# A hybrid encoder block on one core: the begin rewritten (V's products split by kind and interleaved, first weights in three loads, high parts of rows on GpSimd)

## The chip, the cores and the metric

The kernel runs on one core of one Trainium2 chip. The metric is the device time of one execution in microseconds; the median of three runs of the kernel before is 1219.09 us (1218.88 to 1220.08).

## The reference

One encoder layer on 1024 tokens of width 1024, all in float32. In outline:

```
u = rms_norm(x, norm1_g)
proj = u @ w_in                 # q, k, v (512 each), cb, cc, ch (512 each), ga, gb (1024 each)
q, k = per-head rms_norm of q, k (8 heads x 64)
y_a = neighbourhood_attention(q, k, v, rpb) @ w_attn_branch   # 8 x 16 window on a 16 x 64 grid
y_b = (cb * conv3(cc * ch)) @ w_conv_branch
x = x + (sigmoid(ga) * y_a + sigmoid(gb) * y_b) @ w_o
x = x + relu(rms_norm(x, norm2_g) @ w_mlp_in)^2 @ w_mlp_out
```

## The kernel before, in words

Float32 products are made of float16 ones. Every operand is written as a high part (rounded to float16, scaled by a power of two) and a low part (what is left), and a product is three TensorE passes: high by high, high by low, low by high (`PASSES`, L464). The high part is one instruction (`ACTIVATE` on ACT, or `TENSOR_SCALAR` on GpSimd), the low part one `SCALAR_TENSOR_TENSOR` on DVE that reads the high part.

**Rows.** The tokens are eight blocks of 128, called rows here and numbered from 0. `norm` (L435) makes a row's `u`: sum of squares on ACT (L438), a short chain of DVE instructions with one root on ACT (`rstd`, L411 to L420), the high part (L442 on GpSimd for rows 1 to 3, L444 on ACT for the others), the low part on DVE (L446). It is a generator, and `ln_step(b, n)` issues the next n pieces of row b. Rows 0 to 2 are transposed by TensorE with copies out of PSUM (`ln_trans`, L448: high part copied by ACT, L456, low by DVE, L458); rows 3 to 7 by a DMA from SP's queue (`ln_turn`, L461). `u16` has four slots, row b uses slot b mod 4.

**Weights.** A `Chunk` (L242) is a slice of the weights: V has two chunks of 256 columns, Q and K one of 512, each in pieces of 512 KB that SP loads into five `raw` buffers (L232; the next load is issued once a piece's low parts are on DVE). `prep` (L252) finds a scale (by largest value or by sum of squares, L263 on ACT), sums it over the partitions with a product by ones (L201) that DVE reads (L204), turns it into a power of two, scales the rows' gains (L279), and then makes the high parts (L310, ACT) and low parts (L301, DVE) piece by piece.

**Order.** The order on each engine is that in which this Python program issues. Two lists of generators are stepped along with TensorE's work: `fg` (`step`, finishing work of rows and units, the s splits) and `bg` (`tick`, the weights' `prep`). `units` counts finished groups of 24 products; several generators wait in this count (`apart`). A unit's results are read out of PSUM when the next unit has been issued (`settle`); for V this is L534 (ACT) and L535 (DVE).

**The begin, L540 to L596.** V's chunk 0 is prepared, then each of rows 0 to 2 gets a group of 24 products with 256 columns (128x256), then the same rows with chunk 1, then rows 3 to 7 one group each with both chunks (128x512). Q's chunk is prepared meanwhile and Q's groups follow directly (L654). Also in this stretch `sforms` (L491) makes, for later use, sums and differences of x's halves: for a pair of rows n and n + 4 ACT scales both (L499), GpSimd does four `TENSOR_TENSOR` (L503), and later ACT and DVE split the result (`s`, L508 and L510). `SFORM` (L489) gives the count of units from which each may be issued.

TensorE's banks are `d` (3), `s` (3) and `o` (2).

Of the kernel before, what the change touches and what calls it, by code (L numbers as in the profile page):

```python
# [52 lines left out]
def encoder_block(ctx: ExitStack, tc: tile.TileContext, x, weights, cols, gqk, rel, masks, out):  # L53
# [128 lines left out]
    def apart(mark, n=3, of=units):  # L182
        while of[0] < mark + n and not forced[0]:
            yield WAIT
# [57 lines left out]
    class Chunk:  # L242


        def __init__(self, kind, widths, tag, rows, half, more):
            self.kind, self.bank = kind, {"V": "o", "Q": "o", "K": "s", "C": "d"}.get(kind)
            self.tag, self.rows, self.widths, self.more = tag, rows, widths, more
            self.offs = []
            self.raw, self.ready, self.half = [], more > 0, half
            self.split = False  # L250

        def prep(self):  # L252
# [5 lines left out]
            if self.kind in "QKCG" or self.half:  # L258
                self.parts = vhome[0][:, 1] if self.half else wsp.tile([128, 2, tot], F16, name="w16_ws", tag="ws")
# [10 lines left out]
                if self.half:  # L270
                    yield
                else:
                    yield from apart(units[0], 2 if self.kind == "Q" else 3)
                yield from all_sum(c, b, bank(self.bank) if self.bank else anybank(), 1e-36, not self.half)
# [8 lines left out]
            if self.half is not None:  # L283
                if not self.half:
                    vhome.append(wsp.tile([128, 2, 2, tot], F16, name="w16_v", tag="ws"))
                self.parts = vhome[0][:, self.half]
            elif self.kind not in "QKCG":
                self.parts = wpool[self.tag].tile([128, 2, tot], F16, name="w16_" + self.tag, tag=self.tag)
# [27 lines left out]
        def largest(self, rm, a, b):  # L316
            o = 0
# [15 lines left out]
            if self.kind != "V":  # L333
                yield from apart(units[0], 3 if self.kind != "O" else 1 + (self is cO[1]))
            yield from all_sum(c, b, bank(self.bank) if self.bank else anybank(), 1e-30, self.kind != "V")
# [112 lines left out]
    def ln_trans(u16, b, dst):  # L448
        for s in range(2):
            pt = bank16("o")  # L450
            for k in range(8):
                T.transpose(pt[:, k * 128:(k + 1) * 128], u16[:, s, k * 128:(k + 1) * 128], ident)
            o = dst[:, s, :, b * 128:(b + 1) * 128]
            i = pt.rearrange("p (k t) -> p k t", k=8)
            if s == 0:
                A.activation(o, i, AF.Copy)  # L456
            else:
                V.tensor_copy(o, i)  # L458

# [25 lines left out]
    ln = [norm(xt[:, b], sq, u16[:, b % 4], at(ys, b), 0 < b < 4) for b in range(8)]  # L485
# [42 lines left out]
    def v_unit(b, j, steps, ticks):  # L528
        ps = bank("ds"[b % 2])
        n, c = (512, 0) if j is None else (256, 256 * j)  # L530

        def post():
            hi, lo = (VT[:, b, s, c:c + n] for s in range(2))
            A.activation(hi, ps[:, :n], AF.Copy, scale=2.0 ** -20)  # L534
            V.scalar_tensor_tensor(lo, ps[:, :n], 2.0 ** -20, hi, op0=OP.mult, op1=OP.subtract)  # L535
        w = vhome[0] if j is None else vhome[0][:, j]
        unit(group(ps[:, :n], [(UT[:, sa, k, b * 128:(b + 1) * 128], w[..., sw, k * 256:(k + 1) * 256])
                               for k in range(8) for sa, sw in PASSES]), post, steps, ticks)
# [1275 lines left out]
```

## Time and profile before

| | |
|---|---|
| median of three runs | 1219.09 us |
| the profiled execution | 1219.86 us, of which its span is 1218.0 us |
| granted TensorE clock | 1.0 throughout |
| PE busy over the span | 98% |
| DVE, ACT, POOL busy over the span | 76%, 63%, 35% |
| chain that ended last, by engine | PE 74%, DVE 15%, ACT 5%, DMA 3%, issue 2% |

PE is TensorE's products, PEld its weight loads, POOL is GpSimd, SP issues DMAs. A row of the timeline gives start, duration, engine, line, operation, output and inputs, shapes, how many such instructions are merged in the row, and in brackets how long the engine was idle before it and what ended this. Where several are merged the duration is that of all. A row of the table by stage gives the stretch, its length, the busy time of PE, PEld, DVE, ACT and POOL, each with its number of instructions, then clock, DMA share and GB/s. A row of the chain that ended last gives start, duration and what was worked on.

### The profile page before, as it was taken

What the parts mean: (1) busy time and instruction counts of PE and PEld (TensorE: products, weight loads), DVE (VectorE), ACT (ScalarE), POOL (GpSimd) and SP (SyncE); (2) the same over time, 40 slices, a digit from 0 to 9 for tenths busy, and PEclk for the clock granted to TensorE, in tenths of its full rate; (3) what the DMA queues carried; (4) which work ended last, traced back from release to release, by engine and by line L of the source; (5) the groups of instructions that cost most, each with busy time, mean ns of one, the idle gap of its engine ahead of it and who ended that gap; (6) DMA issues with size and microseconds to landing.
All of it is one profiled execution on the core that took longest, in us unless ns stands there. A gap on an engine that the chain in (4) does not pass through costs nothing.

```text
span 1218.0 us, 17069 instructions
## 1 busy us (share of the span) xinstructions
PE 1194.1 (98%) x6294; PEld 572.9 (47%) x6294; DVE 931.3 (76%) x1758; ACT 764.4 (63%) x1186; POOL 423.2 (35%) x276
## 2 busy tenths in 40 slices
PE   5999999999999999999999999999999999999998
PEld 4544444454444444444458444444444444444444
DVE  6667878898468686887877665456448989998997
ACT  6786677777545455436668787687776754646440
POOL 1430003231411111101003465655657472553562
PEclk9999999999999999999999999999999999999999
DMA  7558555756651121226095654355375835335302
GB/s 279 106 186 182 113 124 114 154 111 118 133 143 54 51 69 35 70 62 246 19 184 131 208 190 160 129 187 166 129 284 199 314 127 203 143 134 195 104 35 104
DMA packets 170867, 173.35 MB, mean 142 GB/s; under 512 B 131488, under 2 KB 132000, under 8 KB 166688
## 3 DMA queue, kind: packets, MB, share of 16 engines
q1 hardware_dynamic: 170208, 168.07, 47.6%
q10 hardware_dynamic: 576, 4.19, 0.9%
q8 instruction: 49, 0.80, 0.3%
q14 instruction: 34, 0.28, 0.1%
HBM read 102.51 MB, written 37.75 MB: 115 GB/s over the span
## 4 chain that ended last, share of the span: by engine, by line
PE 74%; DVE 15%; ACT 5%; DMA 3%; issue 2%; SPq 0%; POOL 0%; ACTq 0%; DVEq 0%
PE ps_d L210 26%; PE ps_s L210 23%; PE ps_o L210 16%; PE ps_d L911 7%; DVE w_s L1033 2%; PE ps_s L831 1%; PE ps_o L888 1%; DVE w_ws L301 1%; DMA qD<-q 1%; DVE s L510 1%; DVE u L446 1%; DVE sg L1149 1%; DMA u2T<-v 1%; ACT w_ws L263 1%; DVE w_v L301 1%
## 5 line engine op out<-in xcount | busy, mean ns | idle before, releaser
L210 PEld LDWEIGHTS <-ops 128*128 128x128 f16 x1356 | 132.4, 98 | 157.3
L210 PEld LDWEIGHTS <-w 128*128 128x128 f16 x1368 | 132.8, 98 | 140.5 <-DMA u2T<-v 1.0
L911 PE MATMUL ps_d<-uT,w_ws 128*128 128x512 f16 x528 | 125.0, 379 | 0.0
L210 PE MATMUL ps_d<-ops 128*128 128x512 f16 (+1 forms) x528 | 118.3, 374 | 0.0
L1635 ACT ACTIVATE ops<-hf,sc 128x2048 f16<-128x2048 f32 x26 | 52.0, 2002 | 98.5 <-PE ps_o L210 35.9
L210 PE MATMUL ps_s<-ops 128*128 128x512 f16 x492 | 112.9, 379 | 0.0
L1022 POOL TENSOR_TENSOR tsum<-raw 128x512 f32<-128x512 f32 x28 | 45.8, 1648 | 148.9 <-ACT raw L1008 148.9
L210 PEld LDWEIGHTS <-uT 128*128 128x128 f16 x648 | 63.4, 99 | 68.2 <-issue 5.4
L1215 POOL TENSOR_TENSOR as<-as 128x512 f32<-128x512 f32 x56 | 77.5, 1385 | 40.8 <-ACT as L1495 37.5
L210 PEld LDWEIGHTS <-w_s 128*128 128x128 f16 x588 | 56.8, 98 | 69.5 <-DVE w_s L1033 2.0
L210 PE MATMUL ps_d<-u2x,w 128*128 128x512 f16 (+1 forms) x360 | 80.0, 372 | 0.0
L210 PE MATMUL ps_o<-ops 128*128 128x512 f16 x336 | 77.1, 379 | 0.0
L911 PEld LDWEIGHTS <-w_ws 128*128 128x128 f16 x528 | 51.0, 98 | 52.8
L1637 DVE SCALAR_TENSOR_TENSOR ops<-hf,sc,ops 128x2048 f16<-128x2048 f32 x26 | 72.6, 2791 | 3.5 <-ACT ops L1635 3.5
L1008 ACT ACTIVATE raw<-raw,sc 128x256 f32<-128x256 f32 x172 | 71.1, 496 | 1.9 <-DMA raw<-in_weights 1.9
L210 PE MATMUL ps_o<-u2T,w 128*128 128x512 f16 (+1 forms) x324 | 71.7, 371 | 0.0
L1022 POOL TENSOR_TENSOR gsum<-raw 128x512 f32<-128x512 f32 x14 | 19.0, 1377 | 133.8 <-issue 73.7
L1037 ACT ACTIVATE w<-raw,sc 128x512 f16<-128x512 f32 (+1 forms) x28 | 24.7, 929 | 52.3 <-DVE sc L431 52.3
L210 PE MATMUL ps_s<-u2T,w 128*128 128x512 f16 (+1 forms) x252 | 52.7, 359 | 0.0
L854 ACT ACTIVATE sz<-sz,sc 128x384 f32<-128x384 f32 (+1 forms) x64 | 37.4, 584 | 24.3 <-DVE sc L845 12.5
L1528 DVE TENSOR_TENSOR as<-ps_d,as 128x512 f32<-128x512 f32 (+1 forms) x14 | 9.4, 672 | 55.6 <-ACT as L1547 53.5
L310 ACT ACTIVATE w_ws<-raw,sc 128x512 f16<-128x512 f32 (+2 forms) x72 | 41.0, 638 | 15.6 <-DVE sc L279 15.6
(340 smaller groups left out, 2616.8 us busy)
## 6 DMA issues: line engine op xcount, KB each, us to landing
raw<-in_weights SPq DMA_DIRECT2D x89, 512.0 KB, 5.8
hs<-as SPq DMA_DIRECT2D x16, 1792.0 KB, 8.8
hf<-hs SPq DMA_DIRECT2D x26, 1024.0 KB, 6.7
w2x<-in_weights SPq DMA_DIRECT2D x16, 512.0 KB, 8.3
raw<-in_weights SPq DMA_DIRECT2D x16, 384.0 KB, 3.7
xt<-in_x SPq DMA_DIRECT2D x8, 512.0 KB, 10.1
gs<-s ACTq DMA_DIRECT2D x4, 1024.0 KB, 4.6
x<-in_x SPq DMA_DIRECT2D x8, 512.0 KB, 9.7
```

The costliest lines, as they stand in the source:

```text
L210: T.matmul(ps, l, r, start=a, stop=b)
L301: V.scalar_tensor_tensor(lo, self.raw[p][:, o:o + m], sc[:, c:c + 1], hi, op0=OP.mult, op1=OP.subtract)
L310: A.activation(self.parts[:, 0, f + o:f + o + m], self.raw[p][:, o:o + m], AF.Copy, scale=sc[:, c:c + 1])
L854: A.activation(z, z, AF.Exp, scale=-1.0, bias=sc[:, d["mx"]], accum_out=sc[:, d["sm"]])
L911: T.matmul(ps, l, r, start=a, stop=b)
L1008: A.activation(v, v, AF.Copy, scale=sc[:, at(g, 4 * i + k)])
L1022: G.tensor_tensor(t[:, o], a, b, op=OP.add)
L1033: V.scalar_tensor_tensor(o(1), w, sc[:, s], o(0), op0=OP.mult, op1=OP.subtract)
L1037: A.activation(o(0), w, AF.Copy, scale=sc[:, s])
L1215: sub.tensor_tensor(z[o], z[a], z[b], op=op)
L1635: A.activation(P[:, 1, 0], hf, AF.Copy, scale=sc[:, Rs])
L1637: V.scalar_tensor_tensor(P[:, 1, 1], hf, sc[:, Rs], P[:, 1, 0], op0=OP.mult, op1=OP.subtract)
```

## The change

Only the begin is rewritten, with the helpers that it calls.

- The second piece of V's chunk 0 is loaded in two halves (so the first weights come in three loads), and the search for the largest value follows the loads (4 + 2 + 2 slices).
- The begin's order is written out by hand: `turn_row` (half of the former `ln_trans`), `v_part` (high or low parts of some slices), `v_mms` (products of some slices and passes), `v_post`. V's products go by kinds: high by high, low by high and high by low of rows 0, 1, 2 are apart and interleaved with transposes, and three groups (one for each of rows 0, 1, 2) are open in three banks at a time.
- Rows 1 to 7 make their high part on GpSimd (before: rows 1 to 3).
- The norms of rows 4 to 7 are issued ahead of the products of row 3; before, they were issued one by one between the products.
- Q's chunk is pushed once, before the last passes of V's chunk 1, with two ticks ahead of row 3's product; before, it got two ticks at each of three groups.

The core of the diff (left out: the branches of `prep` and `largest` for V that are no longer used, `ln_trans`, and `v_unit`'s half form; `HH`, `HL`, `LH` are the three passes):

```
     def load_into(t, ch, p):
         m = ch.widths[p][0] * ch.widths[p][1]
-        SP.dma_start(t, bass.AP(tensor=weights.tensor, offset=weights.offset + ch.offs[p], ap=[[m, 128], [1, m]]))
+        n = m // (1 + (ch.half == 0 and p == 1))
+        for o in range(0, m, n):
+            SP.dma_start(t[:, o:o + n], bass.AP(tensor=weights.tensor, offset=weights.offset + ch.offs[p] + o,
+                                                ap=[[m, 128], [1, n]]))
...
-    ln = [norm(xt[:, b], sq, u16[:, b % 4], at(ys, b), 0 < b < 4) for b in range(8)]
+    ln = [norm(xt[:, b], sq, u16[:, b % 4], at(ys, b), b > 0) for b in range(8)]
...
+    def turn_row(b, s):
+
+        pt = bank16("o")
+        for k in range(8):
+            T.transpose(pt[:, k * 128:(k + 1) * 128], u16[:, b, s, k * 128:(k + 1) * 128], ident)
+
+        def copy():
+            o, i = UT[:, s, :, b * 128:(b + 1) * 128], pt.rearrange("p (k t) -> p k t", k=8)
+            if s == 0:
+                A.activation(o, i, AF.Copy)
+            else:
+                V.tensor_copy(o, i)
+        return copy
+
+    def v_begin(ch):
+        ch.rm, ch.a, ch.b, ch.s = (cols_of("prep", i) for i in (8, 1, 1, 1))
+        ch.inv = keep()
+
+    def v_sum(ch, c):
+        ch.sum = bank("o")
+        T.matmul(ch.sum[:, 0:1], ones[:, 0:128], c, start=True, stop=True)
+
+    def v_scale(ch, floor, power):
+        V.tensor_scalar(sc[:, ch.b], ch.sum[:, 0:1], floor, None, op0=OP.max)
+        for _ in power:
+            pass
+        V.tensor_scalar(sc[:, ch.rm], sc[:, g1], sc[:, ch.s], None, op0=OP.mult)
+
+    def v_part(ch, s, ks):
+        for k in ks:
+            p, o = k // 4, k % 4 * 256
+            hi, lo = (ch.parts[:, w, k * 256:(k + 1) * 256] for w in range(2))
+            raw, c = ch.raw[p][:, o:o + 256], sc[:, at(ch.rm, k)]
+            if s == 0:
+                A.activation(hi, raw, AF.Copy, scale=c)
+            else:
+                V.scalar_tensor_tensor(lo, raw, c, hi, op0=OP.mult, op1=OP.subtract)
+                if k % 4 == 3:
+                    done[0] += 1
+                    load_upto(done[0] + 5)
+
+    vps, vn = {}, {}
+
+    def v_mms(b, j, ks, *passes):
+        if (b, j) not in vps:
+            vps[b, j], vn[b, j] = bank("ds"[b % 2]), 0
+        for k in ks:
+            for sa, sw in passes:
+                n = vn[b, j] = vn[b, j] + 1
+                T.matmul(vps[b, j][:, :256], UT[:, sa, k, b * 128:(b + 1) * 128],
+                         vhome[0][:, j, sw, k * 256:(k + 1) * 256], start=n == 1, stop=n == 24)
+        if n == 24:
+            units[0] += 1
+
+    def v_post(b, j, s):
+        hi, lo = (VT[:, b, w, 256 * j:256 * j + 256] for w in range(2))
+        if s == 0:
+            A.activation(hi, vps[b, j][:, :256], AF.Copy, scale=2.0 ** -20)
+        else:
+            V.scalar_tensor_tensor(lo, vps[b, j][:, :256], 2.0 ** -20, hi, op0=OP.mult, op1=OP.subtract)
+
+    HH, HL, LH = PASSES
+    lower, upper, eight = range(4), range(4, 8), range(8)
     V.tensor_reduce(sc[:, gm2], sc[:, g1], axis=AX, op=OP.max, apply_absolute_value=True)
     mul(gm2, gm2, gm2)
-    push(cV[0])
+    v0, v1 = cV
+    vhome.append(wsp.tile([128, 2, 2, 2048], F16, name="w16_v", tag="ws"))
+    for j in range(2):
+        v_begin(cV[j])
+        cV[j].parts = vhome[0][:, j]
     ln_step(0, 7)
-    tick()
+    for k, n in (0, 4), (4, 2), (6, 2):
+        V.tensor_reduce(sc[:, at(v0.rm, k, n)], v0.raw[k // 4][:, k % 4 * 256:(k % 4 + n) * 256].rearrange(
+            "p (k w) -> p k w", k=n), axis=AX, op=OP.max, apply_absolute_value=True)
+    turn_row(0, 0)()
+    mul(v0.rm, g1, v0.rm)
+    V.tensor_reduce(sc[:, v0.a], sc[:, v0.rm], axis=AX, op=OP.max, apply_absolute_value=True)
+    c = ones_col()
+    V.tensor_copy(c, sc[:, v0.a])
+    v_sum(v0, c)
     ln_step(1)
-    tick(3)
+    v_scale(v0, 1e-30, pow2(v0.b, 14, v0.s, v0.inv, False, v0.more))
     ln_step(0)
+    v_part(v0, 0, (0,))
     ln_step(1)
-    tick(4)
-    ln_trans(u16[:, 0], 0, UT)
+    v_part(v0, 0, range(1, 8))
     ln_step(1, 5)
-    flush()
-    v_unit(0, 0, 0, 0)
+    turn_row(0, 1)()
+    v_part(v0, 1, lower)
+    v_mms(0, 0, range(7), HH)
+    copy = turn_row(1, 0)
+    v_mms(0, 0, (7,), HH)
+    copy()
+    v_mms(0, 0, eight, LH)
+    v_mms(0, 0, lower, HL)
     ln_step(2)
-    push(cV[1])
-    tick()
+    ln_step(1)
+    v_mms(1, 0, eight, HH)
+
+    def v1_square(p):
+        A.activation(v1.parts[:, 1, 1024 * p:1024 * p + 1024].bitcast(BF16), v1.raw[p], AF.Square,
+                     accum_out=sc[:, at(v1.rm, p)])
+
+    v1_square(0)
     ln_step(2)
-    tick()
-    ln_step(1)
+    v1_square(1)
+    v_part(v0, 1, (4, 5))
+    turn_row(1, 1)()
     ln_step(2, 5)
-    tick()
-    ln_trans(u16[:, 1], 1, UT)
-    tick(7)
-    v_unit(1, 0, 0, 0)
+    v_mms(0, 0, (4, 5), HL)
+    v_mms(1, 0, eight, LH)
+    v_part(v0, 1, (6, 7))
+    v_mms(0, 0, (6, 7), HL)
+    v_mms(1, 0, eight, HL)
+    V.tensor_reduce(sc[:, v1.a], sc[:, at(v1.rm, 0, 2)], axis=AX, op=OP.add)
+    c = ones_col()
+    V.tensor_tensor(c, sc[:, v1.a], sc[:, gm2], op=OP.mult)
+    copy = turn_row(2, 0)
+    v_sum(v1, c)
+    copy()
+    ln_step(2)
+    v_scale(v1, 1e-36, pow2_half(v1.b, 14, v1.s, v1.inv, v1.more))
+    v_part(v1, 0, lower)
+    v_post(0, 0, 0)
     ln_step(3)
-    ln_step(2)
-    tick()
-    ln_trans(u16[:, 2], 2, UT)
+    v_mms(2, 0, eight, HH)
+    turn_row(2, 1)()
+    v_mms(2, 0, eight, HL)
+    v_mms(2, 0, eight, LH)
+    v_post(0, 0, 1)
+    v_part(v1, 1, lower)
+    v_part(v1, 0, (4, 5))
     ln_step(3)
-    tick()
-    ln_step(3, 4)
+    v_part(v1, 0, (6, 7))
+    v_post(1, 0, 0)
+    ln_step(4)
+    ln_step(3, 5)
+    v_post(1, 0, 1)
+    v_part(v1, 1, (4, 5))
+    ln_step(3)
+    ln_turn(u16[:, 3], 3, UT)
+    v_part(v1, 1, (6, 7))
+    for ks in lower, upper:
+        for b in range(3):
+            v_mms(b, 1, ks, HH, LH)
+    ln_step(4)
+    v_post(2, 0, 0)
+    ln_step(5)
+    ln_step(4, 5)
+    v_post(2, 0, 1)
+    ln_step(5)
+    ln_step(6)
+    ln_step(4)
+    ln_turn(u16[:, 0], 4, UT)
+    turned[0] = 5
+    ln_step(5, 5)
     fg.append(qk_gain())
     fg.append(sforms())
-    for p in range(11):
-        if p == 3:
-            flush()
-            push(cQ)
-        if p == 1:
-            step()
-            tick(2)
-        elif p and p < 6:
-            v_unit(p % 3, p // 3, 1, 2)
-        elif p > 5:
-            v_unit(p - 3, None, 0, 4 if p < 7 else 8)
-        for q in (p,) if p < 6 else (2 * p - 6, 2 * p - 5):
-            c = q // 2 + 3
-            if c < 8 and q % 2 == 0:
-                ln_step(c, 2)
-                ln_turn(u16[:, c % 4], c, UT)
-                turned[0] = c + 1
-            if c < 7:
-                ln_step(c + 1, 3)
-        if p > 5:
-            step(2)
+    push(cQ)
+    for b in range(3):
+        v_mms(b, 1, eight, HL)
+    ln_step(6)
+    ln_step(7)
+    ln_step(5)
+    ln_turn(u16[:, 1], 5, UT)
+    turned[0] = 6
+    ln_step(6, 5)
+    for b in range(3):
+        v_post(b, 1, 0)
+        v_post(b, 1, 1)
+    ln_step(7)
+    tick(2)
+    ln_step(6)
+    ln_turn(u16[:, 2], 6, UT)
+    turned[0] = 7
+    ln_step(7, 5)
+    step(2)
+    for b in range(3, 8):
+        v_unit(b, 4 if b < 4 else 8)
+        if b == 3:
+            ln_step(7)
+            ln_turn(u16[:, 3], 7, UT)
+            turned[0] = 8
+        step(2)
     settle()
     flush()
```

From here on an instruction of the change is named by its line in the changed kernel; L306 there is L310 before, L297 is L301, L482 is L499, L491 is L508, L493 is L510, L516 and L517 are L534 and L535, L441 is L446.

DVE, from row 2's transposed low part to row 3's low part. Before, with `vT` V's result, `u_81` the rows' u, `w_v` V's low parts, `gq` the gains of q and k:

```order
L458 COPY uT<-ps_o 128x8x128
L411 TENSOR_SCALAR sc<-sc 128x1
L301 SCALAR_TENSOR_TENSOR w_v<-raw,sc,w_v 128x256 x4
L414 RECIPROCAL sc<-sc 128x1
L416 SCALAR_TENSOR_TENSOR sc<-sc 128x1
L102 TENSOR_TENSOR sc<-sc 128x1
L420 SCALAR_TENSOR_TENSOR sc<-sc 128x1
L446 SCALAR_TENSOR_TENSOR u_81<-xt,sc,u_81 128x1024
```

The same place in the change:

```order
L532 COPY uT<-ps_o 128x8x128
L580 SCALAR_TENSOR_TENSOR vT<-ps_d,vT 128x256
L557 SCALAR_TENSOR_TENSOR w_v<-raw,sc,w_v 128x256 x4
L406 TENSOR_SCALAR sc<-sc 128x1
L409 RECIPROCAL sc<-sc 128x1
L411 SCALAR_TENSOR_TENSOR sc<-sc 128x1
L102 TENSOR_TENSOR sc<-sc 128x1
L415 SCALAR_TENSOR_TENSOR sc<-sc 128x1
L580 SCALAR_TENSOR_TENSOR vT<-ps_s,vT 128x256
L557 SCALAR_TENSOR_TENSOR w_v<-raw,sc,w_v 128x256 x2
L441 SCALAR_TENSOR_TENSOR u_81<-xt,sc,u_81 128x1024
```

Two of V's results and two more low parts of V's weights now stand ahead of row 3's low part.

ACT, from V's result of row 3 on. Before, with `s_559` the split of the pair of rows 0 and 4, `s_653` that of rows 1 and 5, `w_ws` Q's weights, `xt` the rows of x that are scaled for the next pair:

```order
L534 ACTIVATE vT<-ps_s 128x512
L444 ACTIVATE u_81<-xt,sc 128x1024
L508 ACTIVATE s_559<-xt 128x4x512
L534 ACTIVATE vT<-ps_d 128x512
L310 ACTIVATE w_ws<-raw,sc 128x512 x4
L534 ACTIVATE vT<-ps_s 128x512
L310 ACTIVATE w_ws<-raw,sc 128x512 x4
L499 ACTIVATE xt<-xt,sc 128x1024 x2
L508 ACTIVATE s_653<-xt 128x4x512
```

The same place in the change, where `s_639` is the split of rows 1 and 5:

```order
L516 ACTIVATE vT<-ps_s 128x512
L491 ACTIVATE s_559<-xt 128x4x512
L516 ACTIVATE vT<-ps_d 128x512
L516 ACTIVATE vT<-ps_s 128x512
L306 ACTIVATE w_ws<-raw,sc 128x512 x4
L482 ACTIVATE xt<-xt,sc 128x1024 x2
L491 ACTIVATE s_639<-xt 128x4x512
L498 DMA gs<-s_559 128x4096
L516 ACTIVATE vT<-ps_d 128x512
L306 ACTIVATE w_ws<-raw,sc 128x512 x4
```

Q's high parts come one of V's results later, and the scaling of the next pair and the second split now stand between their first and second half.

DVE at the same place. Before, from the first split to the second:

```order
L510 TENSOR_TENSOR s_559<-xt,s_559 128x4x512
L535 SCALAR_TENSOR_TENSOR vT<-ps_d,vT 128x512
L204 TENSOR_SCALAR sc<-ps_o 128x1
...
L279 TENSOR_SCALAR sc<-sc 128x8
L301 SCALAR_TENSOR_TENSOR w_ws<-raw,sc,w_ws 128x512 x2
L535 SCALAR_TENSOR_TENSOR vT<-ps_s,vT 128x512
L301 SCALAR_TENSOR_TENSOR w_ws<-raw,sc,w_ws 128x512 x6
L510 TENSOR_TENSOR s_653<-xt,s_653 128x4x512
```

In the change:

```order
L493 TENSOR_TENSOR s_559<-xt,s_559 128x4x512
L517 SCALAR_TENSOR_TENSOR vT<-ps_d,vT 128x512
L517 SCALAR_TENSOR_TENSOR vT<-ps_s,vT 128x512
L204 TENSOR_SCALAR sc<-ps_o 128x1
...
L279 TENSOR_SCALAR sc<-sc 128x8
L297 SCALAR_TENSOR_TENSOR w_ws<-raw,sc,w_ws 128x512 x2
L493 TENSOR_TENSOR s_639<-xt,s_639 128x4x512
L517 SCALAR_TENSOR_TENSOR vT<-ps_d,vT 128x512
L297 SCALAR_TENSOR_TENSOR w_ws<-raw,sc,w_ws 128x512 x6
```

The second split and one of V's results moved from behind Q's eight low parts to between the second and the third.

More of the change, by code (lines that the diff above doesn't have):

```diff
@@ L257, in prep @@
             tot = sum(k * w for k, w in self.widths)
[L258 to L259 removed]
+            if self.kind in "QKCG":
+                self.parts = wsp.tile([128, 2, tot], F16, name="w16_ws", tag="ws")
                 for p, (k, w) in enumerate(self.widths):
@@ L269, in prep @@
                 V.tensor_tensor(c, sc[:, a], sc[:, gm2], op=OP.mult)
[L270 to L274, printed above, removed]
+                yield from apart(units[0], 2 if self.kind == "Q" else 3)
+                yield from all_sum(c, b, bank(self.bank) if self.bank else anybank(), 1e-36)
                 yield from pow2_half(b, 14, s, self.inv, more=self.more)
@@ L282, in prep @@
                 yield WAIT
[L283 to L287, printed above, removed]
+            if self.kind not in "QKCG":
                 self.parts = wpool[self.tag].tile([128, 2, tot], F16, name="w16_" + self.tag, tag=self.tag)
@@ L526, in qk_gain, with v_unit @@
         yield from gain(g, 11, sgq, isgq)
-    def v_unit(b, j, steps, ticks):
+    def v_unit(b, ticks):
         ps = bank("ds"[b % 2])
-        n, c = (512, 0) if j is None else (256, 256 * j)
         def post():
[L533 to L538, printed above, removed]
+            hi, lo = (VT[:, b, s] for s in range(2))
+            A.activation(hi, ps, AF.Copy, scale=2.0 ** -20)
+            V.scalar_tensor_tensor(lo, ps, 2.0 ** -20, hi, op0=OP.mult, op1=OP.subtract)
+        unit(group(ps, [(UT[:, sa, k, b * 128:(b + 1) * 128], vhome[0][:, :, sw, k * 256:(k + 1) * 256])
+                        for k in range(8) for sa, sw in PASSES]), post, 0, ticks)
```

18 lines of the change are left out of this document (3 added, 15 removed).

## The prediction

> **What bounds the kernel now.** I read the page's first part, the table by stage, and then the chain that ended last.
>
> ```profile
> PE 1194.1 (98%) x6294; PEld 572.9 (47%) x6294; DVE 931.3 (76%) x1758; ACT 764.4 (63%) x1186; POOL 423.2 (35%) x276
> ```
>
> ```profile
> 0.00:10.00 10.00, 0.00 (x0) 0.10 (x1) 4.25 (x15) 4.40 (x7) 0.44 (x5) 1.00 0.77 285
> 10.00:20.00 10.00, 7.72 (x57) 5.56 (x56) 9.26 (x30) 9.17 (x20) 1.74 (x2) 1.00 0.93 372
> 20.00:30.00 10.00, 8.08 (x78) 6.91 (x79) 7.34 (x23) 7.28 (x18) 2.10 (x2) 1.00 0.52 193
> 30.00:40.00 10.00, 9.19 (x71) 6.93 (x71) 5.59 (x21) 7.44 (x16) 0.00 (x0) 1.00 0.78 160
> 140.00:300.00 160.00, 157.33 (x1112) 77.14 (x1110) 138.35 (x414) 121.90 (x285) 30.41 (x44) 1.00 0.62 125
> 300.00:1218.00 918.00, 912.40 (x4519) 431.61 (x4517) 691.05 (x1086) 543.59 (x735) 359.62 (x206) 1.00 0.44 140
> ```
>
> PE's busy time is the first number with a count behind it: PE is idle for 10.0 + 2.3 + 1.9 + 0.8 = 15.0 us of the first 40 us and for 9 us of all the rest. The change edits only the first 65 us, and behind them the order of every engine is unchanged, so two things can move the end: when PE becomes continuous, and whether it stays so. The chain, which is followed back from the end, says more:
>
> ```profile
> 53.98 3.28 DVE s L510
> 69.20 3.02 DVE s L510
> 94.60 7.00 DMA qD<-q
> ```
>
> PE itself hardly waits in these stretches, yet the chain there runs over DVE's splits of s and over transposes: the engines that feed PE are as late as PE itself. A PE that is delayed in this stretch gets part of it back where it waits for them later:
>
> ```profile
> 108.91 2.58 PE L210 MATMUL ps_d<-w_ws,uT 128*128 128x512 f16 x11 [0.53 <-DVE w_ws L301]
> 164.52 0.48 PE L831 MATMUL ps_s<-kD,qD 128*128 128x384 f16 x2 [0.86 <-DVE sc L845]
> 185.85 0.48 PE L831 MATMUL ps_s<-kD,qD 128*128 128x384 f16 x2 [1.55 <-DVE sc L845]
> ```
>
> **Step 1: from the start to the fourth row's product.** PE is continuous from V of row 3 on (rows counted from 0).
>
> ```profile
> 37.45 5.34 PE L210 MATMUL ps_s<-w_v,uT 128*128 128x512 f16 x24
> 32.21 2.78 PE L210 MATMUL ps_s<-w_v,uT 128*128 128x256 f16 x24
> 12.44 3.29 ACT L310 ACTIVATE w_v<-raw,sc 128x256 f16<-128x256 f32 x8
> 13.83 4.03 DVE L301 SCALAR_TENSOR_TENSOR w_v<-raw,sc,w_v 128x256 f16<-128x256 f32 x8
> 14.01 1.60 POOL L442 TENSOR_SCALAR u<-xt,sc 128x1024 f16<-128x1024 f32 x1 [12.94 <-DVE sc L420]
> 24.88 1.66 DVE L301 SCALAR_TENSOR_TENSOR w_v<-raw,sc,w_v 128x256 f16<-128x256 f32 x4
> 26.47 0.15 DVE L414 RECIPROCAL sc<-sc 128x1 f32<-128x1 f32 x1
> 27.04 0.16 DVE L420 SCALAR_TENSOR_TENSOR sc<-sc 128x1 f32<-128x1 f32 x1
> 27.30 1.12 POOL L442 TENSOR_SCALAR u<-xt,sc 128x1024 f16<-128x1024 f32 x1 [6.31 <-DVE sc L420]
> 28.45 1.29 DVE L446 SCALAR_TENSOR_TENSOR u<-xt,sc,u 128x1024 f16<-128x1024 f32 x1 [1.25 <-POOL u L442]
> 29.77 2.04 SPq L461 DMA_TRANSPOSE uT<-u  x1
> DMA to landing us min/median/max: 4.2/4.2/5.0
> ```
>
> I lay the changed order down with these prices: 0.40 us for each low or high part of a weight, 0.83 us from a row's reciprocal to GpSimd's start, 1.12 there, 1.3 for DVE's low part, 0.109 per 256-column product (2.78 / 24 with the last one's drain taken off), 4.2 from a transpose's issue to its landing. The second weight load in halves lets the reduction end some 0.3 us sooner, and the sum follows; its extra issue on SP stands ahead of row 1's x, which ACT does not want before it has copied row 0's transposes. ACT then stalls: its second instruction behind the first high part is row 1's root, whose input stands on DVE behind row 0's low part (until 12.1), so the other seven high parts end at 15.3, about as before. DVE does four low parts until 15.9 (0.5 of it waiting for GpSimd, as in the 1.60 row), row 1's low part until 17.1, but then row 2's only until 24.0, since the low parts 4 to 7 and the second chunk's sum stand ahead of it, and row 3's until 33.25 (28.45 + 1.29 = 29.7 before), because six low parts of the second chunk and two of V's own are now ahead of it on DVE. PE's own queue is done earlier than before: the three first groups at 27.6, the high products of the three second ones by 33, their last group (which needs the last weight's low part, 34.0) at 36.05. But row 3's product needs row 3's transpose: 33.3 + 4.2 = 37.5. That is the start of before. **Term 1: 0** (from -1.4, if only PE's queue binds, to +0.9 with a landing of 5.0 us).
>
> [...]
>
> **Step 2: rows 4 to 7.** Four high parts leave ACT for GpSimd.
>
> ```profile
> 33.62 1.28 DVE L446 SCALAR_TENSOR_TENSOR u<-xt,sc,u 128x1024 f16<-128x1024 f32 x1 [0.76 <-ACT u L444]
> 46.53 1.29 DVE L446 SCALAR_TENSOR_TENSOR u<-xt,sc,u 128x1024 f16<-128x1024 f32 x1 [0.61 <-ACT u L444]
> ```
>
> On DVE each of rows 4 to 6 takes 0.83 + 1.12 + 1.3, about 3.2 us: low parts from 36.4, 39.6 and 42.7 (rows 4 and 6 began at 33.6 and 46.5 before). Their transposes land at 41.9, 45 and 48, ahead of their products at 42.7, 47.9 and 53.1. ACT's time for these parts was off the path. No term. Row 7's low part now stands behind the sum of Q's squares (about 49.5), its transpose lands near 56, before 58.3. No term either, with 2 us to spare.
>
> **Step 3: Q's weights, the term that decides.** Before, all of Q's high and low parts were ahead of the second s split (the rows quoted with the change). Now ACT scales two x rows and splits s between the first four high parts and the last four, and DVE does that s split between low parts 2 and 3.
>
> ```profile
> 35.37 1.05 ACT L263 ACTIVATE w_ws<-raw 128x1024 bf16<-128x1024 f32 x1
> 43.02 2.18 ACT L499 ACTIVATE xt<-xt,sc 128x1024 f32<-128x1024 f32 x2
> 45.27 14.45 POOL L503 TENSOR_TENSOR xt<-xt 128x512 f32<-128x512 f32 x8 [16.86 <-ACT xt L499]
> 51.70 1.91 ACT L508 ACTIVATE s<-xt 128x2048 f16<-128x2048 f32 x1
> 53.90 3.35 DVE L510 TENSOR_TENSOR s<-xt,s 128x2048 f16<-128x2048 f32 x1
> 58.71 1.04 DVE L279 TENSOR_SCALAR sc<-sc 128x8 f32<-128x8 f32 x1
> 60.41 1.94 ACT L310 ACTIVATE w_ws<-raw,sc 128x512 f16<-128x512 f32 x3
> 63.47 5.34 PE L210 MATMUL ps_d<-w_ws,uT 128*128 128x512 f16 x24
> 63.47 4.06 DVE L301 SCALAR_TENSOR_TENSOR w_ws<-raw,sc,w_ws 128x512 f16<-128x512 f32 x6
> 69.20 3.01 DVE L510 TENSOR_TENSOR s<-xt,s 128x2048 f16<-128x2048 f32 x1 [1.67 <-ACT s L508]
> 72.13 0.68 DVE L535 SCALAR_TENSOR_TENSOR vT<-ps_d,vT 128x512 f16<-128x512 f32 x1
> 76.05 0.67 ACT L612 ACTIVATE qs<-ps_d,sc 128x512 f32<-128x512 f32 x1
> 82.07 2.29 DVE L510 TENSOR_TENSOR s<-xt,s 128x2048 f16<-128x2048 f32 x1 [1.39 <-ACT s L508]
> ```
>
> Before, Q's low parts ran neck and neck with PE (4.06 us for six beside PE's 5.34 for eight steps). Now, in order: row 7's root on ACT at 42.6, two squares of Q to 44.9, two x rows to 47.0; GpSimd's first four sums from 47.05, 1.36 each and about 1 us lost to row 7's low part, to 53.5 (before they began at 45.27); s high to 55.4; s low with GpSimd running beside it, 3.0, to 58.4 (2.29 in the 82.07 row without); V's low parts of rows 4 and 5, 0.6 each, to 59.6; Q's sum and scale, 0.93 up to L279's place and then behind one GpSimd sum, 60.9; four high parts to 63.4; two x rows 65.5; s high 67.4; s low with its wait 70.4; row 6's V 71.0; then six low parts, 4.0 beside nothing and about 6.5 between GpSimd's sums. PE reaches Q at 37.5 + 5 x 5.2 = 63.5, does two of eight steps, and wants the third low part at 64.9, which comes after 71.7. Q's first product, which ended at 68.6, ends 0.5 behind the last low part. With no wait for GpSimd anywhere in this list that is 72.9, or +4.2; with one at each place, 78.5, or +9.9. The rows of before nearest to it (3.35 and 3.01 for the split against 2.29, 1.04 for a scale of eight numbers) carry such waits, so I take the upper half: **term 2: +8.0**.
>
> **Step 4: what is given back.** ACT was late at this point anyway: it read Q's first product at 76.05, 7.4 us after PE had made it. It now gets there at about 79 (K's third weights are loaded later, behind Q's low parts). So the feeding engines move by some 3 us and PE by 8, and PE's waits of before that are quoted above, 0.53 us at K's first product and 0.86 + 1.55 in the attention blocks, vanish. **Term 3: -3.0** (0 if they move as far as PE; hardly more, since the rest of PE's 9 us is split into shorter waits after 300 us).
>
> Sum: 0 + 8.0 - 3.0 = +5.0 us on the profiled execution of 1219.86 us (span 1218.0 and 1.86 around it), 0.8 above the median of the three runs. On the median: 1219.09 + 5.0 = **1224.1 us**.
>
> **Rivals.** (a) Q arrives in time, and the change is not slower. It decides where the third low part of Q comes by 64.9, 7 us sooner than I lay it down. For it: ACT has four high parts less, and DVE sat idle for whole microseconds around each of them. Against it: two ACT and one DVE instruction sets that were behind Q are now in front of it. Then only the start counts: -1.4 (PE's queue binds, row 3 turned by 36.0), 1217.7; if DVE's first 33 us are also 2 us shorter than laid down, 1215.7. (b) The stall comes, but the shorter one, +4.2, and 3.0 of it is given back: +1.2, 1220.3. (c) The stall comes and nothing is given back, because Q's later reads shift with PE: +8.0, 1227.1; with the longer stall 1229. (d) The change does not do what its words say: by my list row 4 is turned later than before (36.4 against 33.6) and row 3 by 3.5 us; this is in term 1, and a landing of 5.0 us adds 0.9 to the start, but nothing to the end, since Q is later still.
>
> **How the numbers follow.** The measurement tells about 0.2% from no change, 2.4 us. The forecast (slower by 2.4 to 7) has 0.50; (c) 0.15, slower; (b) and the mild form of (a), within 2.4 us, 0.22; the strong form of (a), faster, 0.13. So slower 0.65, same 0.22, faster 0.13. The range leaves out about 0.1 on each side: 1216.5 to 1227.5.
>
> **What would show it.** Row 3's product starts at 37 to 38 behind a transpose. DVE's scale of Q stands at 60 to 62. Q's first product stretches from 63.5 to beyond 73, its PE idle time released by DVE's low parts at L297, with the split of s ahead of them. The waits at K's first product and in the first attention blocks are gone. I am wrong in the mechanism if PE runs through Q without a gap, and in the size if ACT's first read of Q's product shifts by as much as PE.

## The result, and the profile after

The changed kernel takes **1230.62 us** (median of five, 1228.43 to 1231.59), the kernel before 1219.89 (median of its five runs beside them): a ratio of 1.0085, 95% interval 1.0074 to 1.0096, or **+10.7 us**. The forecast was slower, by 5.0; the time lies 3.1 us above the end of the range. The profiled execution took 1228.43 us (span 1226.7), the lowest of the five and 8.57 above the profiled execution of before; most readings below are of this pair, and a second profile of the changed kernel (1231.10 us) shows where part of the other 2 us comes from.

The page's first line, and the table by stage with the same columns as before, two stretches added:

```profile
PE 1196.2 (98%) x6294; PEld 572.8 (47%) x6294; DVE 936.1 (76%) x1759; ACT 759.9 (62%) x1182; POOL 429.8 (35%) x280
```

```profile
0.00:10.00 10.00, 1.20 (x9) 0.88 (x9) 4.32 (x16) 4.80 (x7) 0.44 (x5) 1.00 0.80 294
10.00:20.00 10.00, 7.34 (x59) 5.44 (x60) 8.43 (x25) 8.79 (x20) 1.12 (x1) 1.00 0.94 360
20.00:30.00 10.00, 8.76 (x86) 7.37 (x84) 7.70 (x25) 6.47 (x16) 2.08 (x2) 1.00 0.46 156
30.00:40.00 10.00, 8.22 (x59) 5.49 (x58) 7.26 (x20) 5.57 (x15) 2.88 (x3) 1.00 0.97 164
...
60.00:70.00 10.00, 6.33 (x30) 2.75 (x29) 4.91 (x5) 9.70 (x13) 5.07 (x4) 1.00 0.44 157
70.00:80.00 10.00, 6.18 (x16) 1.90 (x16) 10.00 (x8) 5.57 (x9) 8.97 (x6) 0.66 0.60 210
```

TensorE (PE) is idle for 8.8 + 2.7 + 1.2 + 1.8 = 14.5 us of the first 40, against 15.0 before: the rewritten start gained half a microsecond up to row 3. In 60 to 80 it is idle for 7.5 us, and in 70 to 80 VectorE (DVE) is busy without a pause. In the kernel before TensorE had no gap there:

```profile
70.00:80.00 10.00, 10.00 (x48) 4.51 (x47) 5.60 (x7) 7.91 (x13) 9.57 (x7) 1.00 0.50 201
```

The chain that ended last in the changed kernel goes through that place:

```profile
55.02 2.75 DVE s L493
70.39 9.46 DVE w_ws L297 x6
80.48 5.18 PE ps_o L210 x24
```

The timeline of the changed kernel at the places that the prediction named, from row 3's product to the second wait in the attention:

```profile
36.97 5.35 PE L210 MATMUL ps_s<-w_v,uT 128*128 128x512 f16 x24 [1.61 <-DMA uT<-u]
...
43.90 5.35 PE L210 MATMUL ps_d<-w_v,uT 128*128 128x512 f16 x24 [1.58 <-DMA uT<-u]
...
59.83 0.44 DVE L279 TENSOR_SCALAR sc<-sc 128x8 f32<-128x8 f32 x1
...
61.06 1.42 DVE L297 SCALAR_TENSOR_TENSOR w_ws<-raw,sc,w_ws 128x512 f16<-128x512 f32 x2 [0.79 <-ACT w_ws L306]
...
62.77 2.17 ACT L482 ACTIVATE xt<-xt,sc 128x1024 f32<-128x1024 f32 x2
64.66 1.67 PE L210 MATMUL ps_d<-w_ws,uT 128*128 128x512 f16 x7
64.85 1.89 ACT L491 ACTIVATE s<-xt 128x2048 f16<-128x2048 f32 x1
65.02 14.27 POOL L486 TENSOR_TENSOR xt<-xt 128x512 f32<-128x512 f32 x8 [4.78 <-ACT xt L482]
...
66.77 3.01 DVE L493 TENSOR_TENSOR s<-xt,s 128x2048 f16<-128x2048 f32 x1 [4.30 <-ACT s L491]
...
70.31 9.53 DVE L297 SCALAR_TENSOR_TENSOR w_ws<-raw,sc,w_ws 128x512 f16<-128x512 f32 x6
...
71.51 1.44 PE L210 MATMUL ps_d<-w_ws,uT 128*128 128x512 f16 x3 [5.18 <-DVE w_ws L297]
...
79.89 0.59 PE L210 MATMUL ps_d<-w_ws,uT 128*128 128x512 f16 x2 [0.87 <-DVE w_ws L297]
...
174.54 0.48 PE L941 MATMUL ps_s<-kD,qD 128*128 128x384 f16 x2 [0.63 <-DVE sc L955]
...
195.88 0.48 PE L941 MATMUL ps_s<-kD,qD 128*128 128x384 f16 x2 [1.55 <-DVE sc L955]
```

Row 3's product starts at 36.97 behind its transpose (37.45 before), row 4's waits 1.58 us more for its own. Q's third low part starts at 70.31, behind ACT's scaling (L482), its high part of `s` (L491) and DVE's split (L493); the last six take 9.53 us beside GpSimd's eight sums (4.06 before), and PE gets the last six of its eight steps one by one. Q's first product ends at 80.48 instead of 68.81, **11.7 us** later. The same products of the attention start 10.02 and 10.03 later (164.52 and 185.85 before), and the span is 8.7 longer: 3.0 us are given back behind Q.

### The profile page after: what moved, and what is told of

It reads as the page before. It is cut to its first block, busy times and chain, and to the rows that moved or that the text cites. A ratio compares the mean times of both kernels' runs of the same rounds, so it can differ in the third digit from the quotient of the medians.

```text
span 1226.7 us, 17075 instructions
## 1 busy us (share of the span) xinstructions
PE 1196.2 (98%) x6294; PEld 572.8 (47%) x6294; DVE 936.1 (76%) x1759; ACT 759.9 (62%) x1182; POOL 429.8 (35%) x280
## 4 chain that ended last, share of the span: by engine, by line
PE 81%; DVE 11%; ACT 3%; issue 2%; DMA 2%; POOL 1%; ACTq 0%; DVEq 0%; POOLq 0%
PE ps_d L210 28%; PE ps_s L210 22%; PE ps_o L210 19%; PE ps_d L1021 8%; DVE w_s L1143 2%; PE ps_o L998 1%; PE ps_s L941 1%; DVE w_ws L297 1%; DMA xt<-in_x 1%; DVE sg L1259 1%; DMA u2T<-v 1%; POOL xt L486 0%; ACT w_s L1147 0%; DVE u L441 0%; POOL u L437 0%
## 5 line engine op out<-in xcount | busy, mean ns | idle before, releaser
L210 PEld LDWEIGHTS <-uT 128*128 128x128 f16 x504 | 49.2, 98 | 72.8 <-issue 11.7
L210 PE MATMUL ps_o<-u2T,w 128*128 128x512 f16 (+1 forms) x324 | 71.7, 371 | 0.0
L297 DVE SCALAR_TENSOR_TENSOR w_ws<-raw,sc,w_ws 128x512 f16<-128x512 f32 (+2 forms) x72 | 50.8, 757 | 4.0 <-ACT w_ws L306 4.0
L210 PE MATMUL ps_d<-w_ws,uT 128*128 128x512 f16 x192 | 45.7, 391 | 7.5 <-DVE w_ws L297 7.5
```

What stands on the lines that cost most here:

```text
L210: T.matmul(ps, l, r, start=a, stop=b)
L297: V.scalar_tensor_tensor(lo, self.raw[p][:, o:o + m], sc[:, c:c + 1], hi, op0=OP.mult, op1=OP.subtract)
```

## The experiments

Every kernel is timed in rounds with the kernel before on the same chip. Ratios are to that, with their 95% interval. SFORM's triples are the count of finished units from which it may be issued, the row, and 0 for scaling and sums or 1 for the split.

**Q's parts ahead of everything.** The changed kernel with two entries of the table set back:

```
-    SFORM = (..., (10, 2, 0), (10, 1, 1), (11, 3, 0), ...)
+    SFORM = (..., (11, 2, 0), (11, 1, 1), (11, 3, 0), ...)
```

> The changed kernel, with the scaling of pair 2 (L482) and the split of s in rows 1 and 5 (L491, L493) set back behind all eight of Q's weight parts, as before the change; nothing else differs. Theory T (what stands between Q's weight parts makes nearly all of the loss): the waits of 5.18 us and 2.31 us on Q's low parts go, Q's row 0 ends near 72 instead of 80.3, and the whole is near 1221 us (1219 to 1223), that is within 0.3% of the kernel before; the 1.6 us waits for rows 3 and 4 at TensorE stay. Rival R1 (the loss is made in the new order of V or by the high parts on GpSimd, and Q only shows it): the time stays at 1227 or more, and the waits reappear at another place ahead of 105 us.

Measured: 1220.43 us (1219.62 to 1221.20), ratio 1.0006 (0.9997 to 1.0015). Its timeline:

```profile
60.16 0.44 DVE L279 TENSOR_SCALAR sc<-sc 128x8 f32<-128x8 f32 x1
...
64.31 4.06 DVE L297 SCALAR_TENSOR_TENSOR w_ws<-raw,sc,w_ws 128x512 f16<-128x512 f32 x6
64.76 5.34 PE L210 MATMUL ps_d<-w_ws,uT 128*128 128x512 f16 x24
...
68.28 12.52 POOL L486 TENSOR_TENSOR xt<-xt 128x512 f32<-128x512 f32 x8 [7.71 <-ACT xt L482]
```

Q's scale comes as late as in the changed kernel, but nothing stands between the parts, GpSimd starts later, the six take 4.06 us, and PE has no gap. Nearly all of the loss is at this place, and R1 is out. What the rest of the change earns is also read here: nothing that can be measured.

**The split alone, and the sums alone.** Two kernels, each with one of the two set back:

```
+    SFORM = (..., (10, 1, 1), (11, 2, 0), (11, 3, 0), ...)     # split alone between Q's parts
+    SFORM = (..., (10, 2, 0), (11, 1, 1), (11, 3, 0), ...)     # sums alone beside Q's parts
```

> The changed kernel, where only the scaling of pair 2 (L482), and with it GpSimd's sums (L486), is set back behind Q's parts; the split of s in rows 1 and 5 still stands between Q's second and third low part on VectorE. So GpSimd is idle during the six low parts. Theory T: both matter. The split has only its own high halves (1.9 us) ahead of it on ScalarE and starts about 2 us sooner, and the six low parts take 4.1 us instead of 9.5: Q's row 0 ends near 73.5, and the time is 1222 to 1224. Rival R2 (GpSimd's sums alone): as without split, within 0.7 us of the run that has all Q's parts ahead. Rival R3 (the split and its wait alone): within 1.5 us of the changed kernel, 1227 to 1231. R1: 1227 or more.

> The changed kernel, where only the split of s in rows 1 and 5 is set back behind Q's parts; the scaling of pair 2 and GpSimd's sums (L486) stand as in the changed kernel. So VectorE's low parts wait for no split, but run beside GpSimd. Theory T: low parts 3 and 4 come ahead of GpSimd's sums, the others beside them at about 1.6 us each, Q's row 0 ends at 73 to 75, and the time is 1222 to 1225. R2 (the sums alone): 1227 to 1231. R3 (the split alone): within 0.7 us of the run that has all Q's parts ahead. R1: 1227 or more.

Measured, the split alone: 1223.81 us (1222.99 to 1225.00), 1.0033 (1.0020 to 1.0045). The sums alone: 1224.90 (1223.19 to 1227.13), 1.0042 (1.0030 to 1.0055). The rows of the first:

```profile
65.62 2.29 DVE L493 TENSOR_TENSOR s<-xt,s 128x2048 f16<-128x2048 f32 x1 [2.22 <-ACT s L491]
...
68.43 6.08 DVE L297 SCALAR_TENSOR_TENSOR w_ws<-raw,sc,w_ws 128x512 f16<-128x512 f32 x6
69.23 5.00 PE L210 MATMUL ps_d<-w_ws,uT 128*128 128x512 f16 x15 [2.45 <-DVE w_ws L297]
70.68 11.60 POOL L486 TENSOR_TENSOR xt<-xt 128x512 f32<-128x512 f32 x8 [9.51 <-ACT xt L482]
```

and of the second:

```profile
65.26 6.30 POOL L486 TENSOR_TENSOR xt<-xt 128x512 f32<-128x512 f32 x4 [4.78 <-ACT xt L482]
...
65.70 0.69 DVE L517 SCALAR_TENSOR_TENSOR vT<-ps_d,vT 128x512 f16<-128x512 f32 x1 [2.98 <-ACT vT L516]
66.31 9.26 DVE L297 SCALAR_TENSOR_TENSOR w_ws<-raw,sc,w_ws 128x512 f16<-128x512 f32 x6
67.13 0.81 PE L210 MATMUL ps_d<-w_ws,uT 128*128 128x512 f16 x3 [0.96 <-DVE w_ws L297]
```

In the first I had expected GpSimd to be idle beside all six parts. It was not: its sums began at 70.68, and the six parts took 6.08 instead of 4.1. Up to the first sum the parts start 0.66 to 0.67 us apart (69.75, 70.42, 71.08), beside the sums the next one starts 1.69 later (72.77), so it is the sums that set the price. In the second no split is ahead of the third low part, but ACT's scaling of `x` still is: the result of V that DVE reads first (L517) waits 2.98 us for ACT, and the third low part starts at 66.31, 2.0 later than with Q's parts ahead. From there on DVE waits for no other instruction that the profile names, and the six still take 9.26. So the sums alone more than double the low parts; the 4.5 us that this run lost contain the late start too. By medians the split alone costs 3.4 us, the scaling with its sums 4.5, and both together 9.2 (1229.65 of the next run less 1220.43): 1.4 more than their sum. R2 and R3, one of the two alone, are out.

**The changed kernel again.**

> The changed kernel once more, unedited. Its five times lay between 1228.4 and 1231.6 and the profile fell on the lowest. All theories: the same median within 1 us. If the low parts beside GpSimd's sums make the spread too, their six take another time in this profile than 9.53 us, and the runs without these sums beside Q's parts have a spread of at most 1 us; if the spread comes from elsewhere (a transfer's landing), the runs without them spread as widely, over 2 us.

Measured: 1229.65 us (1229.41 to 1231.10), 1.0082 (1.0068 to 1.0096). This profile fell on the slowest execution, 1231.10. Six low parts take 9.52 us in it, as in the first profile, and the runs with Q's parts ahead spread over 1.6 us too, so nothing here shows the sums to make the spread. Its rows at the start:

```profile
6.66 1.21 DVE L593 TENSOR_REDUCE sc<-raw 128x4 f32<-128x1024 f32 x1
8.76 1.35 DVE L593 TENSOR_REDUCE sc<-raw 128x2 f32<-128x512 f32 x2 [0.88 <-DMA raw<-in_weights]
```

In the first profile the three reductions ran without a pause (6.80 to 9.20). Here the second waited 0.88 us for its load, and row 3's product began at 39.06. The 2.1 us between 36.97 and 39.06 is most of the difference between the two profiled executions (2.67); the load's wait is one part of it, the rest builds up between 10 and 37.

**The high parts of rows 4 to 7**, first on the base with Q's parts ahead, then in the changed kernel as it is, then by themselves in the kernel before:

```
-    ... at(ys, b), b > 0) for b in range(8)]        # the changed kernel
+    ... at(ys, b), 0 < b < 4) for b in range(8)]    # first and second run; the third is the reverse, in before
```

> As the run with Q's parts ahead (1220.4 us), but the high parts of rows 4 to 8 stay on ScalarE as before the change (1.0 us each there, 1.1 us on GpSimd). Theory T (this part of the change is worth nothing either way): 1219.6 to 1221.2. Rival (the high parts on GpSimd delay row 4's turn or hold up VectorE): row 4's turn is issued over 0.5 us sooner and the time is under 1219.6. Rival (ScalarE was the bound there, so the move was a gain): over 1221.2.

> The changed kernel as it is (1230), but the high parts of rows 4 to 8 stay on ScalarE. Theory P (ScalarE's list up to Q's high parts is on the path, and the high parts on GpSimd take 3 us from it): Q's scale (L279) comes at about 63 instead of 59.8 to 62, the low parts and GpSimd's sums follow as late, and the time is 2 to 4 us above the changed kernel, 1232 to 1234. Rival (the stall is set by the second split and the sums alone): within 1 us of the changed kernel.

> The kernel before, where rows 4 to 7 too make their high part on GpSimd; nothing else of the change. With Q's parts ahead, GpSimd's high parts were worth 4 us (1220.4 against 1224.6). Theory P (the part pays only because the change also issues the norms ahead of the sums): here the high parts of rows 6 and 7 stand behind four sums each (L503, about 1.4 to 1.8 us each from 45.3), row 6's turn lands near 57 for a product that is wanted at 53, row 7's later still, and the time is 1223 to 1229. Rival (the part pays by itself, since ACT is relieved): 1216 to 1219. Rival (worth nothing alone): within 0.8 us of before.

Measured: 1224.59 us (1222.61 to 1224.70), 1.0032 (1.0019 to 1.0044); 1233.39 us (1232.80 to 1233.69), 1.0109 (1.0095 to 1.0123); 1227.39 us (1225.57 to 1229.10), 1.0067 (1.0053 to 1.0080). By medians the parts on ACT cost 4.2 us in the first (against 1220.43) and 3.7 in the second (against 1229.65), by the ratios 3.2 and 3.3, so my expectation of nothing for the first was wrong. The first run's scale and its wait:

```profile
63.23 0.45 DVE L279 TENSOR_SCALAR sc<-sc 128x8 f32<-128x8 f32 x1
...
68.18 3.03 PE L210 MATMUL ps_d<-w_ws,uT 128*128 128x512 f16 x13 [1.44 <-DVE w_ws L297]
```

With 1.1 us more per row (L439, 1.13 to 1.15) ACT reaches the scaling of `x` and the squares of Q later, the sums and the first split follow, and Q's scale comes 3.1 us later (63.23 against 60.16); then the low parts are late even with nothing between them. In the kernel before, the move to GpSimd alone loses 7 us by medians (8 by the ratio), by another mechanism, the one expected:

```profile
44.53 5.31 POOL L503 TENSOR_TENSOR xt<-xt 128x512 f32<-128x512 f32 x4 [6.25 <-ACT xt L499]
...
49.82 1.12 POOL L442 TENSOR_SCALAR u<-xt,sc 128x1024 f16<-128x1024 f32 x1
...
56.58 8.25 PE L210 MATMUL ps_d<-w_v,uT 128*128 128x512 f16 x24 [3.13 <-DMA uT<-u]
```

Row 6's high part stands in GpSimd's queue behind four sums, its transpose lands 3.13 us after PE wanted it, and the product then runs at a lower clock (0.56 in 55 to 60, below); row 7's turn makes PE wait another 1.89. So this part pays in the order of the change, where the norms stand ahead of the sums, and loses in that of before; no run moved the norms by themselves.

**The first weights in two loads**, with Q's parts ahead (`n = m` in `load_into`).

> As the run with Q's parts ahead (1220.4 us), but V's first weights come in two loads as before the change instead of three; the three reductions of the largest values stay. Theory T: the third reduction can begin later by at most the landing of a quarter piece, and one issue of 0.4 us on SP goes; the time is 1220.0 to 1221.2. Rival (the split load brings the first scale, and with it the whole of V, forward by a microsecond): over 1221.2.

Measured: 1220.49 us (1219.79 to 1221.36), 1.0004 (0.9995 to 1.0013). No worth of the third load shows.

**The waits for rows 3 and 4.** Three kernels on the base with Q's parts ahead, each with one step more: K's first load issued after row 4's turn; then row 3's low part and turn ahead of two low parts of the weights; then K's load after row 6's turn.

```
-    v_part(v1, 1, (4, 5))
     ln_step(3)
     ln_turn(u16[:, 3], 3, UT)
+    v_part(v1, 1, (4, 5))                  # moved in the second and third run
     v_part(v1, 1, (6, 7))                  # its load_upto, for K's first load, is left out in all three
...
     ln_turn(u16[:, 0], 4, UT)
+    load_upto(done[0] + 5)                 # and put here, in the third run behind row 6's turn
```

> As the run with Q's parts ahead (1220.4 us), but K's first load (L234), which stood between the turns of rows 3 and 4 on SP's queue, is issued after row 4's turn. That run's row 4 turn was issued at 37.4 and landed at 44.0 (6.6 us; row 3's took 4.4), 1.32 us after TensorE was free. Theory L (the load's bytes stand ahead of the turn's): row 4's turn lands 4.2 to 4.5 us after its issue, at about 41.9, the wait before row 4's product goes, and the time is 1219.0 to 1219.6. Rival (turns issued close together hold each other up, or the turn is as slow whatever is loaded): the wait stays at 1.1 us or more and the time within 0.4 us of 1220.4.

> As the run with K's load after row 4's turn, and besides row 3's low part (L441) and its turn stand ahead of V's fifth and sixth low parts of the second half (L557 x2) on VectorE. In the run with Q's parts ahead GpSimd's high part of row 3 was done at 30.97 and the low part began at 31.56, and the first low-part product of the second half came only at 33.8. Theory: row 3's turn is issued and lands 0.5 us sooner, the wait before row 3's product falls from 1.63 to about 1.1, and the time is 0.3 to 0.6 us below that of the run with K's load later. Rival (the low parts moved back now hold TensorE, or row 4's turn ends the wait instead): no gain, or a wait for w_v (L557) of up to 0.6 us.

> As the run with row 3's low part ahead (1219.7), but K's first load is issued after row 6's turn. With the load ahead of row 4's turn this took 6.5 us to land, with the load right behind it 5.7; in the kernel before, with no load near it, 4.2. Theory L2 (a load in the queues next to a turn holds it up on either side): row 4's turn lands 4.2 to 4.5 us after its issue, the wait of 1.3 us before row 4's product goes, and the time is 1218.4 to 1219.2. Rival (TensorE's gain is given back where the feeding engines bind later): the wait goes, but the time stays within 0.4 us of 1219.7. Rival (the turn is slow by itself): the wait stays over 0.8 us.

Measured: 1220.10 us (1219.33 to 1221.35), 1.0001 (0.9992 to 1.0009); 1219.66 (1219.18 to 1222.00), 0.9998 (0.9989 to 1.0007); 1220.39 (1219.71 to 1221.55), 1.0005 (0.9997 to 1.0014). Row 3's wait fell from 1.63 to 0.83 us in the second, a little more than expected; row 4's, which was to go in the first and the third, was 0.51, 1.29 and 1.32. The times differ by less than their intervals, so no gain of these steps is shown. Row 4's turn in the third, where no load is under way beside it (the nearest were issued at 29.3, landing after 3.6 us, and at 47.0):

```profile
L444 SPq DMA_TRANSPOSE uT<-u x1: 2878/2878/2878, 38.2 to 38.2; - x1
...
DMA to landing us min/median/max: 5.7/5.7/5.7
```

It landed after 6.5 us with K's load ahead of it, 5.7 and 5.9 with the load right behind, and 5.7 without. So the load ahead costs some 0.8 of the 2.3 us above the 4.2 that rows 5 to 7 took before (row 4's own turn took 5.0 there), and theory L2 falls: without a load the turn is still slow. In the DMA view of the last run, 36 to 45 us in 40 slices:

```profile
GB/s 216 197 172 6 0 0 0 0 0 0 0 0 0 0 76 166 208 170 22 0 7 9 10 10 257 289 290 320 273 197 10 121 279 291 261 289 281 256 238 218
```

The turn's bytes start near 39.2, and from 40.1 to 41.4 hardly any move (0 to 22 GB/s); then they go on (257 to 320 GB/s up to 42.5). What holds them there stays open.

**The first split behind Q too**, on the last of these kernels:

```
-    SFORM = (..., (8, 0, 1), (11, 2, 0), ...)
+    SFORM = (..., (11, 0, 1), (11, 2, 0), ...)
```

> As the run with K's load after row 6's turn, and the first split of s (rows 0 and 4; 1.9 us on ScalarE, 2.75 us on VectorE with a wait of 2.6 us ahead of it) is set back behind Q's low parts as well. Theory: Q's scale comes 4 to 5 us sooner (near 56), so that Q's weights can't be late even with TensorE 2 us sooner; TensorE is gapless from row 4 to K; the splits then collide with the reading of Q's first product on ScalarE and VectorE, and the time is within 0.5 us of the run without this. Rival (VectorE has slack there): 0.5 to 1.5 us below it. Rival (Q's first results are read late, and the attention waits for them): 0.5 us or more above it.

Measured: 1218.46 us (1217.12 to 1220.43), **0.9988** (0.9980 to 0.9997). Q's scale comes at 57.98 (60.93 in the run without this; I had expected 56), the six low parts start 3 us ahead of PE's first product of Q, and the waits of 0.53 us at K (110) and of 0.36 at 154, which the run without this has, are gone:

```profile
57.98 1.22 DVE L279 TENSOR_SCALAR sc<-sc 128x8 f32<-128x8 f32 x1
...
62.92 4.05 DVE L297 SCALAR_TENSOR_TENSOR w_ws<-raw,sc,w_ws 128x512 f16<-128x512 f32 x6
...
65.99 5.34 PE L210 MATMUL ps_d<-w_ws,uT 128*128 128x512 f16 x24
```

It is the best kernel of the study, 11 to 12 us below the changed one and, by the ratio, 1.5 us below the one before; that gain is smaller than the 0.2% that I called a difference, though its interval leaves out 1. The move is worth 1.9 us against the run without it. Of the three expectations the slack of VectorE, 0.5 to 1.5 us, is the nearest, and the gain lies beyond it too; the split was not moved alone on any other base.

## Why the direction was right and the size was not

**Term 1 (row 3's start, 0): right.** 36.97 for 37.5, behind a transpose, as laid down; 39.06 in the slower execution, which is beyond the +0.9 that I had allowed.

**Step 2 (rows 4 to 7, no term): right for the sum, wrong in two of its reasons.** Row 4's transpose was to land at 41.9 and landed 6.8 us after its issue at 37.1: a wait of 1.58 us, which costs nothing in the changed kernel, since Q is later still, and leaves it without gain once Q's stall is gone. And "ACT's time for these parts was off the path" is wrong in the order of the change: it sets Q's scale, and with the parts left on ACT the time is 3 to 4 us higher.

**Term 2 (Q's weights, +8.0): the step that failed, by one price in it.** The list came out well: L279 at 59.83 for 60.9, the second split and its wait done by 69.8 for 70.4, the third low part from 70.31 where I had 71.0 to 71.7. The error is "about 6.5 between GpSimd's sums" for the six low parts. They took 9.53, so the term is +11.7 and not +8.0, and lies above my upper bound of +9.9. Of the 3.7 us that it missed, these six parts are 3.0; 1.9 more is that I set the term below its own longer sum, and the list ahead of the six parts gave some 1.2 back by coming sooner. I had priced the sums as a partial disturbance, from rows in which a split beside GpSimd lost 0.7 to 1.1 us in all. That is one wait of one long instruction; six short ones meet six waits. The run with the sums and no split shows that this needs nothing else (9.26), the run with Q's parts ahead that without the sums they take 4.06.

**Term 3 (given back, -3.0): right in size by luck, wrong in place.** The wait of 0.53 us at K is gone, the first in the attention fell from 0.86 to 0.63, but the one of 1.55 stayed at 1.55: the three waits that I had added up to 2.94 gave back 0.76. The shift shrinks in small steps instead: 11.7 at Q, 10.0 in these attention blocks, 8.7 at the end. ACT's first read of Q's product, which I had moved by 3 us, moved by 4.5 (80.52 for 76.05), while PE moved by 11.7; so the engines that feed PE did move less than PE, as the step says, but its size was taken from the wrong waits.

So the profiled pair gives 11.7 - 3.0 = +8.7 for a forecast of +5.0. The median lies 6.5 above the forecast of 1224.1: 3.7 is term 2, about 2.0 that the profiled execution was the lowest of its five, and 0.8 that the kernel before took 1219.89 beside these runs and not 1219.09. Rival (c), a stall of 8 with nothing given back, would have come nearer in the number (1227 to 1229) and is wrong in both parts.

## What to carry to other kernels

When a change puts GpSimd's sums beside short VectorE instructions such as these low parts, count a wait for every one of them, not a share of the whole: here six parts of 0.68 us, 4.06 in all, became 9.53. Moving work between an engine's queue places is priced by what then stands between two parts that TensorE waits for: here two entries of an order table were 9 us, and the whole rewriting around them nothing that could be measured. Test a part on the base in which it would run: the same move to GpSimd gained 3 to 4 us behind early norms and lost 7 to 8 behind four sums.

## What the runs showed of the hardware

**VectorE's low parts and GpSimd's sums take turns.** In the changed kernel the low parts follow each other every 1.6 to 1.7 us (PE's steps, which wait for them, start at 71.51 and 79.89: five intervals of 1.68), with one sum of GpSimd in each interval; alone a part takes 0.68 (4.06 / 6), and a sum alone starts 1.36 after the one before (44.53 to 45.89 in the kernel before with the high parts on GpSimd). In the trace they alternate: the last five parts start at 71.4, 73.1, 74.7, 76.4 and 78.1, the sums beside them at 71.0, 72.6, 74.3, 76.0 and 77.7. A pair takes 1.68, where the two prices alone add up to 2.04. In these five intervals each part lost 1.00 us to a sum, and the 6.5 of my forecast had allowed 0.4.

**TensorE's clock fell behind waits of 2.45, 3.13 and 5.18 us, and not behind 1.89 and 2.15.** The granted clock in the split-alone run, behind its wait of 2.45 us, and in the kernel before with the high parts on GpSimd, behind 3.13 (first stretch) and 1.89 (last):

```profile
68.00:70.00 2.00, 0.77 (x2) 0.26 (x2) 2.00 (x4) 2.00 (x3) 0.00 (x0) 0.77 0.63 262
70.00:72.00 2.00, 2.00 (x6) 0.76 (x5) 2.00 (x3) 2.00 (x3) 1.32 (x1) 0.50 1.05 317
72.00:74.00 2.00, 2.00 (x9) 0.84 (x8) 2.00 (x2) 2.00 (x3) 1.89 (x2) 0.87 0.91 352
```

```profile
55.00:60.00 5.00, 3.42 (x9) 1.22 (x10) 0.69 (x1) 2.40 (x3) 4.76 (x5) 0.56 0.22 40
...
65.00:70.00 5.00, 3.28 (x16) 1.51 (x17) 3.17 (x11) 3.66 (x7) 0.00 (x0) 1.00 0.81 257
```

At 0.50 a product is 0.43 us instead of 0.22, for 3.3 us in the first run (69.23 to 72.55) and 5.9 in the second (56.58 to 62.51); a group of 24 took 8.25 instead of 5.34. The wait of 2.15 us ahead of row 0's second transposes (12.14 in the changed kernel) left the clock at 1.00 as well. The length alone is not shown to decide: the profile gives 1.00 behind the 8.12 us ahead of the first product too, and the fall came 2.3 us after TensorE became idle in the split-alone run (worked out from the mean clock of 0.77 in 68 to 70), but 3.7 after it in the changed kernel, behind the wait of 5.18 (idle from 66.33, clock 0.50 from 70.04). There (0.66 in 70 to 80) DVE's parts came slower than even the slow products, 1.68 us for a part against 1.29 for its three products of 0.43, so the lower clock cost little.

**A transpose by DMA stood nearly still in mid-flight** for 1.3 us (0 to 22 GB/s from 40.1 to 41.4) with no load near (row 4's turn above). The cause was not found.
